# A two-layer trunk with mixers and experts: half of the second layer's modulation taken in one go between the layers

## The chip, the cores and the metric

The kernel runs on one core of a Trainium2 chip. The metric is the device time of one execution in microseconds, as the median of several runs. The profile is of one other execution. Engines are named as in the profile: PE is TensorE (PEld its weight loads), DVE is VectorE, ACT is ScalarE, POOL is GpSimd, SP is SyncE, which issues nearly all DMAs here.

## The reference

Two layers over 256 latent and 256 context tokens, 1024 wide, all in float32. Each layer has a token mixer with four branches and then a mixture of 16 experts, and both are fed by a modulated norm. Cut to what matters here:

```python
for l in range(2):
    mod_x = split((silu(c) @ ada_w[l] + ada_b[l]), 6)       # ada_w[l]: 1024 x 6144
    mod_c = split((silu(c_ctx) @ ada_w[l] + ada_b[l]), 6)
    hx, hc = [rms_norm(x, norm1_g[l]) * (1 + mod[1]) + mod[0] for each stream]
    mc, mx = token_mixer(hc, hx)        # column groups of w_in, two scans, convolution, attention, merge
    xx = xx + mod_x[2] * mx
    hx = rms_norm(xx, norm2_g[l]) * (1 + mod_x[4]) + mod_x[3]
    xx = xx + mod_x[5] * expert_choice_moe(hx)              # 16 experts, 32 tokens each
    # the context stream does the same in the first layer only
```

The six chunks of `mod` are 1024 columns each. Chunks 0 and 1 are needed at the start of a layer's mixer, chunk 2 at its end, and chunks 3, 4 and 5 in the experts.

## The kernel before

All of it stands in one instruction program. Loops are unrolled, and a planner in the compiler orders the instructions of each engine by its own reckoning of when their operands are ready, so that an engine's order can differ from the program text; on the chip each engine then runs its list in order and waits at the first instruction that is not ready. Memory on the chip is handed out by a small allocator (`Mem`, lines 252 to 323) that prefers the piece which has been free for longest.

A modulation chunk is a product of 8 weight tiles (128 x 1024, 512 KB each) with the two conditioning vectors. A tile is loaded by SyncE and used by four matmuls with 32 weight columns each (`Ada.step`, lines 463 to 473), which land in the PSUM tile `pa`; there is one such PSUM buffer. The profile counts a float32 matmul as two pieces, so a tile is 8 pieces of `pa`. After the eighth tile `mod_write` (lines 444 to 454) copies the sums out on VectorE (line 446), transposes them and adds the bias (line 453).

The first layer's chunks 1 and 0 run at the very start, from 16 buffers. The second layer's chunks 1 and 0 run in the background of the first mixer. Its chunks 2 to 5 are the matter here: they are 32 tiles, taken by an `AdaBack` with a pair of 1024-column buffers. It holds a credit, and each call `run(n)` adds n tiles of credit and issues whole tiles:

```python
nxt.append(AdaBack([(1, c) for c in range(2, 6)], keep))   # line 1664, last scatter of the experts
nxt[1].run(TR[0])                                          # line 1666: 0 tiles
ada_bg.run(TR[1])                                          # line 763: 2 tiles, ahead of the modulation
ada_bg.run(TR[2])                                          # line 767: half a tile, 8 times in its loop
ada_bg.run(ADA[l])                                         # line 806: 2 tiles at each weight block
ada_bg.run(SCN[l])                                         # line 934: half a tile per scan level
```

The order of the work around the change is this. The last expert of the first layer gets its weights (line 1608), its outputs are scattered into the token stream (lines 1646 to 1668), and `TokenSums` gathers the sums of squares beside them (lines 542 to 557). `reload` (lines 1670 to 1682) fetches small tables and the first two weight blocks of the next mixer. Then the second mixer begins: the token sums become a reciprocal root on VectorE (lines 498 to 504), it is broadcast by TensorE (line 590), and 16 steps of VectorE, ScalarE and GpSimd modulate the tokens (lines 774 to 780) into a high and a low part. The mixer's products start from these: a small one with `wa` (lines 1009 to 1014), then blocks of `w_in`, each loaded by SyncE (line 803) into one of three raw buffers and split by ScalarE (line 804) and VectorE (line 805). The blocks come in the order of lines 1019, 1022, 1041 (two), then five for the second recurrence with the scan of the first before them (line 1046). Line 1265 finishes what is left of the background ahead of the merge. The mixer's end fetches five tiles of the expert weights ahead (line 1260).

## Time and profile before

| | us |
|---|---|
| median of 3 runs | 2023.9 |
| lowest and highest run | 2020.21, 2026.08 |
| the profiled execution | 2021.9 |
| its span, first to last instruction | 2020.1 |
| TensorE busy | 1859.6 (92%) |
| VectorE busy | 801.5 (40%) |
| ScalarE busy | 526.1 (26%) |
| DMA queue of SyncE, share of 16 engines | 71.2% |
| mean granted TensorE clock, of full | 0.985 |

A slice of the page is a fortieth of the span, 50.5 us. The two stretches in which the DMA engines move 409 GB/s are the experts of the two layers; the second mixer lies between them, from about 1165 us on. A group or row with `pa` in this stretch belongs to the modulation product, `ada_w` to its loads, `wg` to weight blocks of the mixer, `moe_w` to expert weights. Busy matmuls are pipelined, so the busy time of a group can overlap with that of its neighbours.

### The profile page before, as it was taken

The numbers are of one execution on the slowest core, as the hardware profiler recorded it, in microseconds if no ns is written. First come the engines' busy times: TensorE is split into PE (matmuls) and PEld (weight loads), VectorE is DVE, ScalarE is ACT, GpSimd is POOL, SyncE is SP. The second block draws the span as 40 slices with busy tenths as digits, with TensorE's granted clock in tenths as the row PEclk, the third lists the DMA queues.
The fourth block names the chain that finished last, engine by engine and source line by source line (L and its number), as shares of the span: only waits on it lengthen the run. The fifth ranks groups of instructions, "written<-read, shape, count | busy, mean of one in ns | idle before, by whom it ended". The sixth has DMA issues, their size and how long they took to land.

```text
span 2020.1 us, 28474 instructions
## 1 busy us (share of the span) xinstructions
PE 1859.6 (92%) x11722; PEld 1089.5 (54%) x11722; DVE 801.5 (40%) x1768; ACT 526.1 (26%) x929; POOL 28.7 (1%) x52
## 2 busy tenths in 40 slices
PE   7999999999999899999897889999998999987877
PEld 3666677887887434434232356788997333221213
DVE  5464638837543313212020345769865111110101
ACT  4432336622232211101000243447443100000000
POOL 0000000000000000000000010001000000000000
PEclk9998999999999899999999999999998999999999
DMA  8744531322326999999999856334568999999999
GB/s 310 224 151 135 177 102 58 105 84 84 122 98 260 359 401 350 380 409 409 409 409 409 314 188 199 105 102 139 198 251 326 409 409 409 409 409 409 409 409 332
DMA packets 154005, 549.03 MB, mean 272 GB/s; under 512 B 11026, under 2 KB 22674, under 8 KB 153108
## 3 DMA queue, kind: packets, MB, share of 16 engines
q1 hardware_dynamic: 153300, 544.08, 71.2%
q0 software_dynamic: 576, 3.15, 0.5%
q8 instruction: 92, 1.51, 0.3%
q14 instruction: 37, 0.30, 0.0%
HBM read 544.03 MB, written 3.15 MB: 271 GB/s over the span
## 4 chain that ended last, share of the span: by engine, by line
PE 71%; DMA 20%; DVE 5%; issue 2%; ACT 2%; SPq 0%; DVEq 0%; ACTq 0%
PE pd L428 41%; PE ps L428 15%; DMA r<-moe_w 9%; DMA base<-moe_w 7%; PE pm L428 6%; PE pa L428 6%; DMA base<-ada_w 2%; PE pm L425 2%; DMA base<-wg 1%; ACT r L804 1%; PE ps L1597 1%; DVE r L805 1%; DMA base<-xT 0%; DVE r L1195 0%; DVE base L1594 0%
## 5 line engine op out<-in xcount | busy, mean ns | idle before, releaser
L428 PE MATMUL pd<-r 128*128 128x256 f32 (+3 forms) x2976 | 572.3, 363 | 12.0 <-DMA r<-moe_w 7.6
L428 PEld LDWEIGHTS pd<-r 128*128 128x128 f32 (+2 forms) x2976 | 424.7, 184 | 132.0 <-issue 59.3
L428 PE MATMUL pd<-r,r 128*128 128x512 f32 (+3 forms) x1304 | 284.1, 435 | 12.0 <-DMA r<-moe_w 9.4
L805 DVE TENSOR_TENSOR r<-base,r 128x1024 fp32r<-128x1024 f32 x136 | 166.0, 1222 | 160.5 <-ACT r L804 157.4
L428 PEld LDWEIGHTS pd<-r,r 128*128 128x128 f32 (+2 forms) x1304 | 162.7, 167 | 107.6 <-issue 59.3
L804 ACT ACTIVATE r<-base 128x1024 fp32r<-128x1024 f32 x136 | 143.5, 1059 | 268.9 <-PE pd L428 216.2
L428 PE MATMUL ps<-base 32*64 32x64 f32 (+12 forms) x2372 | 178.3, 280 | 12.3 <-DMA base<-hy 4.4
L428 PE MATMUL pd<-r,base 128*32 128x512 f32 (+1 forms) x680 | 166.7, 598 | 12.0 <-DMA r<-moe_w 10.4
L428 PEld LDWEIGHTS ps<-base 32*64 32x64 f32 (+7 forms) x2372 | 113.2, 144 | 73.3 <-issue 43.3
L428 PE MATMUL pm<-base 128*128 128x128 f32 (+12 forms) x660 | 104.7, 326 | 18.3 <-DVE base L1528 5.8
L428 PE MATMUL ps<-r,base 128*64 128x512 f32 (+4 forms) x468 | 98.6, 525 | 13.7 <-DVE base L1598 6.3
L428 PE MATMUL pd<-base 128*32 128x512 f32 (+1 forms) x408 | 100.5, 595 | 6.4 <-DMA base<-moe_w 5.6
L428 PEld LDWEIGHTS pm<-base 128*128 128x128 f32 (+5 forms) x660 | 72.2, 179 | 61.2 <-issue 31.5
L428 PEld LDWEIGHTS pd<-r,base 128*32 128x32 f32 (+1 forms) x680 | 42.0, 122 | 112.1 <-issue 73.9
L1594 DVE TENSOR_TENSOR r<-base,pd 64x512 f32<-64x512 f32 x16 | 10.9, 680 | 214.4 <-PE pd L428 202.2
L1593 ACT ACTIVATE base<-pd 128x512 f32<-128x512 f32 (+1 forms) x32 | 19.0, 594 | 253.7 <-PE pd L428 253.7
L1594 DVE TENSOR_TENSOR base<-base,pd 128x512 f32<-128x512 f32 x16 | 11.0, 688 | 184.6 <-PE pd L428 150.4
L428 PE MATMUL pa<-r,r 128*128 128x512 f32 (+1 forms) x384 | 82.6, 342 | 1.1 <-DVE base L866 1.1
L1644 ACT ACTIVATE base<-ps 32x512 f32<-32x512 f32 (+2 forms) x28 | 14.7, 526 | 252.5 <-PE ps L428 248.0
L1644 ACT ACTIVATE r<-ps 32x512 f32<-32x512 f32 (+2 forms) x32 | 15.4, 480 | 249.9 <-PE ps L428 243.8
L428 PE MATMUL pd<-base,r 128*32 128x512 f32 (+1 forms) x296 | 71.3, 597 | 9.4 <-DMA base<-moe_w 9.4
L428 PE MATMUL pa<-base 128*32 128x256 f32 (+1 forms) x704 | 70.1, 407 | 9.4 <-DMA base<-ada_w 9.2
(241 smaller groups left out, 1633.6 us busy)
## 6 DMA issues: line engine op xcount, KB each, us to landing
r<-moe_w SPq DMA_DIRECT2D x251, 1024.0 KB, 18.2
base<-moe_w SPq DMA_DIRECT2D x131, 1024.0 KB, 17.9
base<-wg SPq DMA_DIRECT2D x152, 512.0 KB, 3.3
base<-ada_w SPq DMA_DIRECT2D x84, 512.0 KB, 4.6
r<-ada_w SPq DMA_DIRECT2D x12, 512.0 KB, 10.3
base<-xT SPq DMA_DIRECT2D x4, 1024.0 KB, 6.2
filters<-r SPq DMA_DIRECT2D x8, 256.0 KB, 4.3
base<-filters POOLq DMA_DIRECT2D x2, 1024.0 KB, 6.4
```

The costliest lines, as they stand in the source:

```text
L425: T.transpose(out, in_, ident)
L428: return T.matmul(out, lhsT, rhs, start=start, stop=stop, **kw)
L804: A.activation(w[0](), raw(), AF.Copy)
L805: V.tensor_tensor(w[1](), raw(), F(w[0]()), op=OP.subtract)
L1593: A.activation(s_(np_=rows), pa[0:rows, :], AF.Silu)
L1594: V.tensor_tensor(h_(np_=rows), s_(np_=rows), pb[0:rows, :], op=OP.mult)
L1597: T.transpose(p[:, q * rows:q * rows + rows], h_(q * 128, n=128, np_=rows), cs("ident", n=rows, np_=rows))
L1644: A.activation(dst, src, AF.Copy)
```

## The change

Chunks 2 and 3 of the second layer leave the background. A new class takes them: at the end of the first layer's experts it gets as many free 1024-column buffers as there are, up to eight, and issues their loads at once; in the second mixer, after the broadcast of the reciprocal root and ahead of the modulation loop, it issues the matmuls of all 16 tiles, and behind each tile the load that takes its buffer next. After it, chunks 4 and 5 go to a pair of buffers in the background, at one tile per weight block where it was two, and with no call in the modulation loop. The weight slots and the saved tokens are given back ahead of the new buffers.

```diff
--- before.py
+++ after.py
@@ -25,11 +25,10 @@
 BASE = 52736 - RA - RB
 ENGS = ('AV', 'AVG')
 
-TR = (0, 2, 0.5)
 SCN = (0.5, 0.5)
 FL = (1, 1)
 DAS = (0.5, 1)
-ADA = (2, 2)
+ADA = (2, 1)
 FIRST = ("gk", "gq")
 AHEAD = ((0, 0), (0, 5))
 
@@ -494,6 +493,34 @@
                 if not self.left:
                     self.buf.free()
 
+    class AdaTurn:
+
+
+        def __init__(self, chunks, bufs):
+            self.tiles, self.bufs, self.issued = [(l, c, k) for l, c in chunks for k in range(KB)], bufs, 0
+            for _ in bufs:
+                self.load()
+
+        def load(self):
+            if self.issued < len(self.tiles):
+                l, c, k = self.tiles[self.issued]
+                S.dma_start(out=self.bufs[self.issued % len(self.bufs)](),
+                            in_=ins["ada_w"][l][128 * k:128 * k + 128, c * 1024:(c + 1) * 1024])
+                self.issued += 1
+
+        def run(self):
+            for i, (l, c, k) in enumerate(self.tiles):
+                if k == 0:
+                    p = ps("a")
+                b = self.bufs[i % len(self.bufs)]
+                for j in range(4):
+                    mm(p[32 * j:32 * j + 32, 0:256], cs_b(k * 32, n=32), b(j * 256, n=256), k == 0, k == KB - 1)
+                self.load()
+                if k == KB - 1:
+                    mod_write(l, c, p)
+            for b in self.bufs:
+                b.free()
+
 
     def rsqrt_small(x, n, y, t):
 
@@ -760,11 +787,10 @@
             b = rs_tokens(sums.tokens(mem), 2, mem)
             rs = bcast_rs(b, 2)
             b.free()
-            ada_bg.run(TR[1])
+            ada_bg.run()
+            ada_bg = AdaBack([(1, 4), (1, 5)], mem.take(2048))
         for k in range(KB):
             t = tmp[k % 2]
-            if l:
-                ada_bg.run(TR[2])
             for s in range(2):
                 c = slice(s * 256, s * 256 + 256)
                 sc_, sh = Ac(k * 2 + s, n=1), mod[l](k * 2 + s, n=1)
@@ -1656,14 +1682,11 @@
                                            op0=OP.mult, op1=OP.add)
                 if not last and gr == 3:
                     if d == 0:
-                        b, keep = [b for b in slots if b.mem is mem][:2]
+                        b = [b for b in slots if b.mem is mem][0]
                         slots.remove(b)
                         spare.append(b)
-                        slots.remove(keep)
                         nxt.append(TokenSums(0, [view(b, 512 * i, 512) for i in range(4)], tag="s"))
-                        nxt.append(AdaBack([(1, c) for c in range(2, 6)], keep))
                     nxt[0].step(d)
-                    nxt[1].run(TR[0])
                 if last and gr == 3:
                     S.dma_start(out=outT[:, d * 256:d * 256 + 256], in_=xk(d, 1))
 
@@ -1690,7 +1713,18 @@
                     gather(gr + 1)
             if gr < 3:
                 scatter(gr)
-        for b in spare + slots + mid + [xg[1]] + gone + Pg + ys:
+        for b in slots + gone:
+            b.free()
+        mem.merge()
+        if not last:
+            bufs = []
+            while len(bufs) < KB:
+                try:
+                    bufs.append(mem.take(1024))
+                except MemoryError:
+                    break
+            nxt.append(AdaTurn([(1, 2), (1, 3)], bufs))
+        for b in spare + mid + [xg[1]] + Pg + ys:
             b.free()
         mem.merge()
         dump(f"xmoe{l}", xb[0]())
```

## Rows read from the trace of the kernel before

**Rows 1.** The page, slices of the span: busy tenths of TensorE; GB/s of the DMA engines.

```profile
PE   7999999999999899999897889999998999987877
...
GB/s 310 224 151 135 177 102 58 105 84 84 122 98 260 359 401 350 380 409 409 409 409 409 314 188 199 105 102 139 198 251 326 409 409 409 409 409 409 409 409 332
```

**Rows 2.** Busy time by stretch: length, PE, PEld, DVE, ACT, POOL, clock, DMA share, GB/s.

```profile
1166.00:1180.00 14.00, 13.27 (x75) 4.18 (x68) 12.44 (x30) 7.75 (x17) 6.44 (x6) 0.89 0.68 219
1138.00:1150.00 12.00, 11.91 (x120) 7.86 (x120) 5.91 (x23) 5.79 (x14) 0.00 (x0) 1.00 0.98 303
1157.00:1186.00 29.00, 25.26 (x139) 9.71 (x138) 18.71 (x51) 9.22 (x19) 6.44 (x6) 0.88 0.61 200
1186.00:1273.00 87.00, 81.33 (x918) 57.40 (x916) 41.81 (x102) 34.68 (x66) 1.46 (x5) 1.00 0.55 183
1273.00:1340.00 67.00, 66.48 (x590) 54.51 (x587) 42.72 (x108) 28.95 (x61) 2.14 (x5) 1.00 0.27 95
```

**Rows 3.** Busy time by stretch of tile pa alone: PE, PEld, DVE, then as above.

```profile
1157.00:1186.00 29.00, 7.38 (x64) 2.32 (x64) 0.43 (x1) 0.88 0.61 200
1186.00:1273.00 87.00, 17.19 (x192) 4.51 (x192) 0.84 (x2) 1.00 0.55 183
...
1166.00:1186.00 20.00, 4.82 (x44) 1.27 (x36) 0.43 (x1) 0.93 0.57 184
```

**Rows 4.** TensorE's waits, 1157 to 1273 us: us in total, times, longest.

```profile
PE pa L428 <- DMA base<-ada_w: 4.5, 5, 2.2
```

**Rows 5.** Groups of TensorE, 1186 to 1273 us: count, busy, mean ns, idle before.

```profile
L428 PE MATMUL pa<-base 128*32 128x256 f32 x192 | 17.3, 390 | 3.8 <-DMA base<-ada_w 3.8
```

**Rows 6.** Timeline, 1157 to 1201 us: start, us, engine, line, count, idle before.

```profile
1157.22 0.84 PE L428 MATMUL pa<-base 128*32 128x256 f32 x10
...
1165.25 1.26 DVE L774 SCALAR_TENSOR_TENSOR base<-base,pm 128x256 f32<-128x256 f32 x3 [1.21 <-PE pm L425]
...
1179.60 0.43 DVE L446 COPY base<-pa 128x256 f32<-128x256 f32 x1 [1.32 <-PE pa L428]
1179.94 0.48 DVE L780 SCALAR_TENSOR_TENSOR r<-base,r 128x256 fp32r<-128x256 f32 x1
...
1191.30 2.36 DVE L805 TENSOR_TENSOR r<-base,r 128x1024 fp32r<-128x1024 f32 x2 [3.38 <-ACT r L804]
...
1200.67 0.64 PE L428 MATMUL pa<-base 128*32 128x256 f32 x8 [2.19 <-DMA base<-ada_w]
```

**Rows 7.** SyncE's DMA issues in order of time, 1142 to 1186 us.

```profile
1141.78 0.85 SPq L1681 DMA_DIRECT2D base<-wg  x2
1142.68 0.42 SPq L1682 DMA_DIRECT2D base<-cn  x1
1143.20 1.52 SPq L466 DMA_DIRECT2D base<-ada_w  x2
1157.21 0.33 SPq L803 DMA_DIRECT2D base<-wg  x1
```

**Rows 8.** SyncE's own waits, 1140 to 1290 us.

```profile
SPq L466 <- PE pa L428: 50.7, 24, 6.6
```

**Rows 9.** Loads of ada_w, 1140 to 1290 us.

```profile
DMA to landing us min/median/max: 3.6/4.6/8.6
```

**Rows 10.** Busy time at the kernel's start, columns as in rows 2.

```profile
22.00:24.00 2.00, 2.00 (x11) 0.56 (x11) 0.08 (x1) 0.27 (x1) 0.00 (x0) 1.00 1.02 408
```

**Rows 11.** Timeline of TensorE at the kernel's start: four tiles in a row.

```profile
38.85 1.91 PE L428 MATMUL pa<-base 128*32 128x256 f32 x32
```

**Rows 12.** Busy time by stretch, around 1162 us, columns as in rows 2.

```profile
1162.00:1164.00 2.00, 0.00 (x0) 0.00 (x0) 1.65 (x11) 0.00 (x0) 0.00 (x0) 0.53 0.96 352
1168.00:1170.00 2.00, 2.00 (x5) 0.73 (x5) 2.00 (x6) 1.72 (x5) 0.87 (x1) 0.76 0.90 332
```

**Rows 13.** The chain in order of time: start, us, what.

```profile
1185.30 4.83 DMA base<-wg
...
1785.73 19.76 DMA r<-moe_w
```

## The prediction

> **What bounds the kernel now.** I read the slices of the page first, then busy time by stretch, the tiles of the modulation product, TensorE's waits, a timeline, SyncE's issue order, and last the chain. TensorE is busy nearly everywhere; the DMA engines are full only while expert weights stream [rows 1]. Between lies the stretch that the change touches, from the first layer's last expert into the second mixer, 1138 to 1340 us. There TensorE is busy 81.3 of 87 us and then 66.5 of 67 while the DMA moves 183 and 95 GB/s [rows 2]: the stretch is TensorE's, and memory has room. Its holes are 29.0 - 25.3 = 3.7 us in 1157 to 1186 and 87.0 - 81.3 = 5.7 us in 1186 to 1273 [rows 2].
>
> The 32 weight tiles of the four modulation chunks (4 matmuls each, seen as 8 pieces) run here: 64 pieces, 8 tiles, before 1186 and 192 pieces, 24 tiles, after it [rows 3]. TensorE stood idle 4.5 us in five waits for such a tile [rows 4], 3.8 us of it after 1186 [rows 5]; the longest, 2.19 us before 1200.67, is one tile with mixer matmuls queued behind it [rows 6]. The reason is the pair of buffers: SyncE issues two tiles at 1143.20 and nothing more until 1157.21 [rows 7], because the next load wants a buffer that TensorE must read first; this kind of wait makes 50.7 us of SyncE's time [rows 8]. One tile takes 3.6 us at least and 4.6 us in the median from issue to landing [rows 9].
>
> **The change part by part.** No matmul, byte or vector instruction is added or removed: 32 tiles and four chunk ends before and after. What moves is when 16 of them run.
>
> *The turn.* Chunks 2 and 3 get every free 1024-column piece, up to eight. I count six: the buffer of the saved tokens has 4096 columns (four pieces), and the weight slot that the pair no longer takes gives two. Six loads then stand behind the reload of the small tables, where now two stand [rows 7]. From 1138 to 1150 the DMA moved 303 GB/s [rows 2]. Four more tiles are 2.1 MB, 5 us at the 408 GB/s that the kernel's first 16 tiles reach [rows 10]: all six land about 1156, before TensorE first has time for one at 1157.22 [rows 6]. The loads cost nothing there; the scatter is what hides them, and without it TensorE would wait those 5 us.
>
> *What it costs TensorE ahead of the mixer.* Eight tiles more than now fall before 1186. A tile run without waits costs 1.91 / 4 = 0.48 us [rows 11]; mixed with other shapes its busy time is 17.19 / 24 = 0.72 us, part of it shared with neighbours [rows 3]. I take 0.55, nearer to the pure one: 8 x 0.55 = 4.4 us added. Two things hide it. One is the 3.7 us of holes [rows 2], above all 1162 to 1164, where no matmul runs while VectorE takes a reciprocal root [rows 12]. The other is the clock: from that hole on it is granted at 0.53, and back at 0.76 in 1168 to 1170 [rows 12], so at the half level, 1.2 GHz, for some 7 us (the mean of 0.88 over 29 us [rows 2] says the same: 2 x 0.12 x 29). Some 5 us of them are busy, and the full level would give back up to 2.5 us. I take 3.0 us hidden in holes and 1.2 us from the clock: +0.2 us net. Bounds: -1.8 (all holes and the whole clock) and +4.4 (nothing hidden).
> The Trainium skill ("TensorE: Matmul & The Clock Gate", Part 1: The HAM clock gate) says that the throttled clock is the default and that activity releases it. The fall behind the hole agrees; no row shows whether these 32-column tiles, put into the hole, hold the clock. By the rule the clock term would be the full 2.5 us and this part -1.1 us.
>
> *The second round of the ring.* Tiles 7 to 16 are loaded only as TensorE frees one of the six buffers, from about 1157.8 on. With the two weight blocks of that place (one stands at 1157.21 [rows 7]) that is 12 x 0.524 = 6.3 MB, 15.4 us at 408 GB/s, and some 3 us until the first lands: the last tile is there about 1176. The modulation's last step ends at 1180.4 [rows 6], and the mixer's first product needs it, so a wait for a late tile mostly falls where TensorE cannot finish anyway. Lower bound 0. Upper bound: if all ten tiles stand ahead of the mixer's matmuls, the other work that TensorE does from 1166 to 1180, 13.3 us [rows 2] less the 4.8 of the tiles [rows 3], is pushed behind, 8.5 us. I take 1.5 us, near the lower end, as the single tile waits are 2.2 us at most [rows 4].
>
> *The background half.* After 1186 there are 16 tiles where there were 24: 8 x 0.55 = 4.4 us less on TensorE (3.8 to 5.8 by the two tile prices). The 3.8 us of waits [rows 5] would be 2.5 us for 16 tiles in proportion; with one tile per weight block, not two, a pair of buffers has twice the time. I take 1.3 us left, 2.5 us saved (bounds 0 and 3.8). In program order both versions finish in the scan of the second recurrence, so nothing later changes.
>
> *The rest.* The calls inside the modulation loop and the zero-rate call in the last scatter go; they only issue tiles counted already. The end of the turn's second chunk, a copy of 0.43 us [rows 6] with two small adds, comes onto VectorE during the modulation, where it is busy 18.7 of 29 us [rows 2]: 0.3 us. The background pair is the same 2048 columns, so the five expert tiles fetched ahead in the mixer should stay.
>
> Sum: +0.2 + 1.5 - 4.4 - 2.5 + 0.3 = -4.9 us. Behind the stretch TensorE has hardly a hole until 1340 [rows 2]; then the expert weights stream at 409 GB/s [rows 1], and the chain ends on them [rows 13]. The stream starts as the mixer gives up its buffers, so it shifts with it and the gain passes through. The profiled execution took 2021.9 us, the span of 2020.1 and 1.8 around it; it would take 2017.0. The median shown, 2023.9, lies 2.0 us above it: 2019.0.
>
> **The rivals.**
> *The hole only moves* (16%). In 1186 to 1273 the tiles are also filler while VectorE runs the scan; if weight blocks are not ready in their place, TensorE idles instead. For it: a weight block needs VectorE before it can be used, 2.36 us for two [rows 6]. Against it: of TensorE's 5.7 us of holes there 3.8 are waits for tiles. It comes out the same if the planner of the instruction order spreads the turn as it spreads the tiles now, so that the change hardly does what it says. The 4.4 us are not won: -4.9 + 4.4 = -0.5, 2023.4 us.
> *More comes back* (20%). All holes and the whole clock ahead of the mixer (-1.8), no late tile (0), the upper tile price (-5.8) and all waits (-3.8) give, with the 0.3 of the copy, -11.1: 2012.8 us. For it: the late tile of 1200.67 also held up what was queued for the first scan.
> *The vector queue is caught* (15%). The end of a chunk is a VectorE copy that waits for the chunk's last tile, and VectorE runs in order. The copy of the first chunk at 1179.60 stands ahead of the last modulation step and made VectorE wait 1.32 us [rows 6]. If the copy of the turn's second chunk stands ahead of the first modulation step (1165.25), the mixer starts when that chunk is complete: at 1176 by the rate above, at 1181 by the 303 GB/s of the reload [rows 2], so 11 to 16 us late. Less the 6.9 us won behind it, that is +4 to +9, in the middle +6.5: 2030.4 us. It decides when the copy waits longer than 6.9 us. For it: in the program text the turn comes ahead of the loop. Against it: the one wait of this kind is short.
>
> *The issue queue is held* (7%). SyncE's ten new buffer waits stand ahead of weight blocks, as 24 waits of this kind do now, 6.6 us at the longest [rows 8]. If the block of 1185.30, which is on the chain [rows 13], comes that much later, it is -4.9 + 6.6 = +1.7: 2025.6 us. Against it: that block waits for the mixer's own first product, and by then the turn's loads are out.
> The Trainium skill ("DMA: Bandwidth & Descriptors", Anatomy of one DMA) has the rule behind this one: a semaphore wait is held on the issuing sequencer and not in the DMA engines. The 50.7 us of SyncE [rows 8] agree.
>
> **How the numbers follow.** About 0.3% (6 us) is what a measurement of this kernel can tell from no change. The forecast holds 42%; its own range, 2014 to 2023, lies on both sides of that bound: 0.19 faster, 0.23 same. The moved hole gives 0.14 same and 0.02 slower (if the ring stalls besides), the larger gain 0.20 faster, the vector queue 0.12 slower and 0.03 same, the issue queue 0.06 same and 0.01 slower. So faster 0.39, same 0.46, slower 0.15. The range, 2011 to 2030, takes in the larger gain whole and half of the vector queue.
>
> **What would show it.** Right: six loads of modulation weights back to back behind the table reload; 16 tiles (128 pieces) before 1186; a shorter clock fall at 1162; fewer and shorter waits for tiles after 1186; the mixer's work after 1200 some 5 us earlier. Wrong: a first modulation step later than 1166 with a chunk's copy ahead of it on VectorE, TensorE waiting more than 3 us for tiles 7 to 16, or idle time in the scan where tiles were.

## The result: 0.6% slower, and the profile after

The changed kernel takes 2034.9 us (median of 8 runs, 2032.65 to 2040.02), the kernel before in the same runs 2023.56 (2016.96 to 2029.6). The ratio is 1.0061, with a 95% interval of 1.0044 to 1.0079. The forecast was 2019.0 and its range ended at 2030: the sign was wrong.

Where the loss arises is read by the start of the same instruction in both traces, counted from the first modulation step (line 774 before):

| instruction | start before | later by |
|---|---|---|
| first result of the mixer leaves PSUM (L1016) | 1185.3 | 1.7 |
| value pair leaves PSUM (L840) | 1203.5 | 7.4 |
| gate of the third recurrence (L1089, last) | 1288.0 | 3.2 |
| attention, first and last row maximum (L1209) | 1367.8, 1411.8 | 3.4, 5.5 |
| merge (L1341) | 1472.9 | 5.2 |
| merged product split (L1364, last) | 1521.6 | 10.5 |
| last scatter of the experts (L1594) | 2002.1 | 10.5 |

So it has three parts: some 3 us in the start of the mixer, where 5 were to be won, 2 us in the attention, and 5 us between 1473 and 1522, where nothing was expected. One trace is not exact to better than 3 us: two of the programs below, table_in_the_way and filters_moved, run the instructions of the kernel before in the same order up to about 1360, and at 1288 they stand 0.4 us earlier and 2.9 us later. Four traces have the full turn and one tile per block, and differ ahead of 1288 in little but addresses: they stand 3.2, 2.2, 3.4 and 1.7 us later (changed, filters_back, layout_kept, kept_but_filters). So the start loses some 2 us rather than 3; that the 5 were not won is sure.

The stretches from 1157 to 1273 as in [rows 2], after the change, and the tiles `pa` alone as in [rows 3]; line 428 before is line 427 now, lines 803 to 805 are 829 to 831:

```profile
1157.00:1186.00 29.00, 26.03 (x174) 9.36 (x166) 17.53 (x49) 7.78 (x17) 5.54 (x7) 1.00 0.66 219
1186.00:1273.00 87.00, 78.42 (x852) 57.91 (x851) 40.55 (x95) 36.20 (x67) 1.44 (x5) 0.96 0.45 152
```

```profile
1157.00:1186.00 29.00, 9.36 (x104) 2.66 (x96) 0.42 (x1) 1.00 0.66 219
1186.00:1273.00 87.00, 12.73 (x144) 3.34 (x144) 0.84 (x2) 0.96 0.45 152
```

Ahead of 1186 the clock no longer falls (1.00, where [rows 2] had 0.88) and 104 pieces run where 64 did. Behind it 48 pieces are gone and 4.5 us of tile time with them (one more tile runs at 1273.33, just outside; with it, it is 40 pieces and 4.0 us), yet TensorE is idle 87.0 - 78.4 = 8.6 us instead of 5.7, and its clock is down 0.04 x 87 = 3.5 us, as much as in the fall at 1162 before (0.12 x 29 = 3.5). In this trace the fall has not gone. It came 37 us later (the clock is 0.51 from 1162 to 1169 before, 0.50 from 1199.4 to 1206.2 after). The place is not fixed by the program alone: filters_moved, in the old order, falls a little in both stretches:

```profile
1157.00:1186.00 29.00, 23.91 (x129) 8.90 (x122) 18.02 (x49) 9.23 (x19) 6.43 (x6) 0.94 0.60 200
1186.00:1273.00 87.00, 81.44 (x891) 57.50 (x890) 40.36 (x99) 34.65 (x66) 1.44 (x5) 0.98 0.55 182
```

TensorE's waits between 1157 and 1273, the two longest lines (compare [rows 4]); the wait for tiles is down from 4.5 to 1.4 us, and a new one, for a block's split, is longer:

```profile
PE pd L427 <- ACT r L830: 2.6, 1, 2.6
PE pa L427 <- DMA base<-ada_w: 1.4, 2, 1.2
```

SyncE's issues, start and length (compare [rows 7]; L507 is the turn, L465 the background, L829 a weight block), and its waits from 1140 to 1190:

```profile
1142.69 34.63 SPq L507 DMA_DIRECT2D base<-ada_w  x16
1177.37 0.90 SPq L465 DMA_DIRECT2D base<-ada_w  x2
1186.16 0.33 SPq L829 DMA_DIRECT2D base<-wg  x1
1192.54 0.33 SPq L465 DMA_DIRECT2D base<-ada_w  x1
1192.97 0.37 SPq L829 DMA_DIRECT2D base<-wg  x1
```

```profile
SPq L507 <- PE pa L427: 21.2, 9, 5.8
SPq L829 <- PE pd L427: 7.8, 1, 7.8
```

All 16 tiles of the turn stand in one run of 34.6 us. Behind it comes a block that must wait 7.8 us for a product of TensorE, because its raw buffer holds `wa` (it waited 5.4 us before, too), then a tile of the background that waits until 1192.54 for one of the pair's buffers, and only behind that the next block. Before, a block left at 1157.21 [rows 7], and these two ahead of the one of 1185.30 [rows 13]:

```profile
1159.61 0.38 SPq L803 DMA_DIRECT2D base<-wg  x1
...
1174.93 0.33 SPq L803 DMA_DIRECT2D base<-wg  x1
```

What becomes of the late blocks is seen on ScalarE. L830 (L804 before) is the split of a block, the 128x1024 lines L1059 to L1062 (L1033 to L1036 before) are the gate of the first scan with two table loads. After:

```profile
1193.43 0.38 ACT L1049 ACTIVATE base<-pd 128x256 f32<-128x256 f32 x1 [3.47 <-PE pd L427]
...
1195.44 1.05 ACT L830 ACTIVATE r<-base 128x1024 fp32r<-128x1024 f32 x1
...
1197.53 1.07 ACT L1059 ACTIVATE base<-base 128x1024 f32<-128x1024 f32 x1
1198.47 1.07 ACT L830 ACTIVATE r<-base 128x1024 fp32r<-128x1024 f32 x1
1199.56 1.28 ACT L1060 ACT_TABLE_LOAD   x1
```

Before:

```profile
1190.21 2.01 ACT L804 ACTIVATE r<-base 128x1024 fp32r<-128x1024 f32 x2 [1.72 <-DMA base<-wg]
...
1194.67 1.08 ACT L1033 ACTIVATE base<-base 128x1024 f32<-128x1024 f32 x1
1195.77 1.28 ACT L1034 ACT_TABLE_LOAD   x1
```

Both blocks of the value pair were split ahead of the gate; now the second one is split inside it. The landing is not all of it: the first block took 3.2 us to land and was there at 1189.3, and ScalarE stood idle for 3.47 us before 1193.43, but in its list the split stands behind that line. Busy time of 1196 to 1205 (columns as in [rows 2]), before and after:

```profile
1196.00:1205.00 9.00, 6.80 (x62) 5.64 (x61) 2.59 (x4) 5.04 (x5) 0.00 (x0) 1.00 0.67 221
```

```profile
1196.00:1205.00 9.00, 5.62 (x57) 3.78 (x50) 3.87 (x4) 8.83 (x13) 0.31 (x1) 0.69 0.88 300
```

ScalarE is busy 8.83 of 9 us, TensorE is idle for 3.4 of them, and the granted clock is 0.69, so for part of the time at the half level of 1.2 GHz. The chain that ended last (start, us, what) runs through ScalarE's list from 1194.3 to 1202.1:

```profile
1197.65 0.94 ACT base L1059
1198.59 0.94 ACT r L830
1199.56 1.28 ACT L1060
...
1236.94 6.34 DMA base<-wg
```

A block's landing is on it only at 1236.94.

The late part: SyncE's issues of expert tiles fetched ahead (L1286, L1260 before, five of them) and of the sixth (L1597, L1571 before). After:

```profile
1468.25 12.44 SPq L1286 DMA_DIRECT2D base<-moe_w  x5
1480.74 1.58 SPq L829 DMA_DIRECT2D base<-wg  x3
1482.44 0.38 SPq L1597 DMA_DIRECT2D base<-moe_w  x1
```

Before:

```profile
1429.35 0.38 SPq L1571 DMA_DIRECT2D base<-moe_w  x1
...
1444.48 0.38 SPq L1260 DMA_DIRECT2D base<-moe_w  x1
...
1468.34 0.38 SPq L1260 DMA_DIRECT2D base<-moe_w  x1
...
1472.71 2.87 SPq L1260 DMA_DIRECT2D base<-moe_w  x3
```

Five tiles leave in one run, and three blocks queue behind it. The allocator hands out other addresses in the second mixer, since six buffers of the turn are taken and given back there and the pair is taken later. The convolution's filter table now lies at column 10928, where the first of the five tiles goes, and its second table (`df` in the program, called the difference buffer in the expectations) at 23728, inside a weight slot. Not all of the 5 us need be this: from 1473 to 1522 the granted clock is 0.93 after and 0.97 before, so up to 0.04 x 49 = 2.0 us of it is clock.

### The profile page after: what moved, and what is told of

The parts are those of the page before. It is cut to its first block, busy times and chain, and to the rows that moved or that the text cites. A ratio compares the mean times of both kernels' runs of the same rounds, so it can differ in the third digit from the quotient of the medians.

```text
span 2030.9 us, 28467 instructions
## 1 busy us (share of the span) xinstructions
PE 1864.0 (92%) x11722; PEld 1095.0 (54%) x11722; DVE 802.4 (40%) x1768; ACT 526.3 (26%) x929; POOL 28.7 (1%) x52
## 4 chain that ended last, share of the span: by engine, by line
PE 70%; DMA 19%; DVE 6%; ACT 3%; issue 3%; SPq 0%; DVEq 0%; ACTq 0%
PE pd L427 41%; PE ps L427 15%; DMA r<-moe_w 9%; PE pm L427 6%; DMA base<-moe_w 6%; PE pa L427 5%; DMA base<-wg 2%; PE pm L424 2%; DMA base<-ada_w 1%; ACT r L830 1%; DVE r L831 1%; PE ps L1623 1%; DVE base L967 0%; DVE r L1221 0%; DVE base L969 0%
## 5 line engine op out<-in xcount | busy, mean ns | idle before, releaser
L830 ACT ACTIVATE r<-base 128x1024 fp32r<-128x1024 f32 x136 | 143.4, 1058 | 272.3 <-PE pd L427 217.3
L427 PE MATMUL pd<-r,base 128*32 128x512 f32 (+1 forms) x680 | 167.0, 597 | 13.0 <-DMA r<-moe_w 10.5
L427 PE MATMUL ps<-r,base 128*64 128x512 f32 (+4 forms) x468 | 99.0, 526 | 13.3 <-DVE base L1624 6.3
L427 PE MATMUL pd<-base,r 128*32 128x512 f32 (+1 forms) x296 | 71.3, 597 | 10.4 <-DMA base<-moe_w 10.4
## 6 DMA issues: line engine op xcount, KB each, us to landing
r<-moe_w SPq DMA_DIRECT2D x251, 1024.0 KB, 18.2
```

What stands on the lines that cost most here:

```text
L427: return T.matmul(out, lhsT, rhs, start=start, stop=stop, **kw)
L830: A.activation(w[0](), raw(), AF.Copy)
```

## The experiments

Every kernel was timed in five rounds beside the kernel before. "Later by" is read from one trace as above, at L840, at L1089 (1288) and at the end. "Split" says whether ScalarE splits both blocks of the value pair ahead of the first 128x1024 line of the gate. The expectations count their shift at 1288 from the last scatter ahead of the mixer, not from the first modulation step; the two differ by half a microsecond at most. A median is over 6 to 12 runs and a trace is one of them, so the two need not agree.

| kernel | median us | ratio, 95% | later by, us | split |
|---|---|---|---|---|
| changed | 2034.9 | 1.0061 [1.0044, 1.0079] | 7.4, 3.2, 10.5 | inside |
| layout_kept | 2026.47 | 1.0012 [0.9999, 1.0025] | 8.8, 3.4, 5.3 | inside |
| table_in_the_way | 2027.41 | 1.0013 [0.9997, 1.0030] | -1.2, -0.4, 0.6 | ahead |
| filters_back | 2033.64 | 1.0048 [1.0028, 1.0068] | 7.0, 2.2, 6.1 | inside |
| filters_moved | 2026.17 | 1.0008 [0.9990, 1.0025] | 2.4, 2.9, 4.4 | ahead |
| kept_but_filters | 2029.77 | 1.0025 [1.0010, 1.0041] | 7.3, 1.7, 5.2 | inside |
| blocks_first | 2029.49 | 1.0035 [1.0017, 1.0053] | 4.2, 2.7, 10.7 | ahead |
| layout_and_blocks | 2029.98 | 1.0021 [1.0004, 1.0037] | 7.3, 2.4, 3.0 | inside |
| ring_on_pool | 2033.15 | 1.0050 [1.0028, 1.0071] | 15.1, 8.8, 10.5 | ahead |
| blocks_on_pool | 2026.29 | 1.0007 [0.9991, 1.0024] | 9.8, 8.1, 9.5 | ahead |
| ring_reused | 2014.24 | 0.9949 [0.9931, 0.9968] | -1.8, -6.9, -6.2 | ahead |
| ring_waits_only | 2016.6 | 0.9953 [0.9930, 0.9976] | -3.1, -6.9, -7.0 | ahead |
| ring_bytes_only | 2022.9 | 0.9984 [0.9966, 1.0001] | 4.6, 3.2, 4.0 | inside |
| pace_two | 2037.08 | 1.0070 [1.0043, 1.0098] | 14.9, 14.0, 13.3 | inside |
| pace_alone | 2036.47 | 1.0046 [1.0024, 1.0068] | -3.2, 6.6, 7.2 | ahead |
| one_chunk | 2024.31 | 0.9994 [0.9976, 1.0012] | -1.2, 0.4, -0.8 | ahead |
| six_tile_turn | 2034.07 | 1.0050 [1.0031, 1.0070] | 4.0, 4.8, 6.5 | inside |
| background_on_pool | 2033.23 | 1.0040 [1.0019, 1.0061] | 8.3, 5.2, 6.4 | ahead |
| before_background_on_pool | 2030.79 | 1.0034 [1.0014, 1.0054] | 1.1, 10.2, 10.4 | ahead |

### Addresses

**layout_kept** is the changed kernel with every buffer of the second mixer at the address that it has in the kernel before.

```diff
+            mem.plan = [tuple(e) for e in PLAN]      # sizes and addresses of the kernel before
-            ada_bg = AdaBack([(1, 4), (1, 5)], mem.take(2048))
+            ada_bg = AdaBack([(1, 4), (1, 5)], ada_bg.keep)
```

> The changed kernel with one thing undone: every buffer that the second layer takes stands at the address it had before the change (the turn's six buffers and the background pair too), so only the turn, its order and the pace are new. Theory A (the loss comes in two places: about 2.4 us where the weight blocks queue behind the turn's loads on SyncE, and 7.5 us later, after 1375 us, because the buffers moved and the filter table of the convolution now stands where the first expert tile is fetched ahead): the later part goes, about 2026 us, ratio to before 1.001; the first fetched-ahead expert tile is issued near 1447 us and not near 1468, and the shift against the kernel before stays at +2.4 us from 1290 us to the end. Rival B (the turn itself causes all of it, the later loss follows from a TensorE that comes late): about 2035 us, ratio 1.006, the shift grows to +9.7 us at 1525 us as in the changed kernel.

The edit does two small things besides: the sums of a chunk are copied into a part of an older buffer, and the turn's buffers are not given back. With that the mixer's first result comes 4.9 us late instead of 1.7, which is made up by 1288.

The ratio falls from 1.0061 to 1.0012, and the late part is gone: from 1473 to 1522 the shift moves from 4.9 to 5.2. The expert tiles leave one by one again (L1611 is the sixth, L1300 the five):

```profile
1435.82 0.38 SPq L1611 DMA_DIRECT2D base<-moe_w  x1
...
1450.95 0.38 SPq L1300 DMA_DIRECT2D base<-moe_w  x1
...
1474.83 0.38 SPq L1300 DMA_DIRECT2D base<-moe_w  x1
```

The early part (3.4 at 1288) stays. So 0.5% of the time, some 10 us by the ratios (0.0049 x 2024) and 5 by the traces, is addresses and the order that the planner makes of them. Which addresses was then tried four ways: the table alone, and the pair of buffers put back, put in the way, and put in the way of layout_kept.

```diff
 # table_in_the_way: the kernel before
+        H = mem.take_span(10928, 2048) if l else mem.take(2048)
 # filters_moved: the kernel before; kept_but_filters: the same two in layout_kept
+        df, H = (mem.take_span(23728, 1024), mem.take_span(10928, 2048)) if l else ...
 # filters_back: the changed kernel
+        df, H = (mem.take_span(14256, 1024), mem.take_span(20656, 2048)) if l else ...
```

> The kernel before with one thing of the change done: in the second layer the filter table of the convolution (2048 columns) is taken at the address of the first expert tile that is fetched ahead, as in the changed kernel. Theory A: that load waits for the convolution's last read of the table, near 1467 us instead of 1444, the fetched-ahead tiles and the weight blocks of the last two merges crowd each other, about +5 us: 2028.5 us, ratio 1.0025. Rival B: the load has room to come late, 2023.6 us, ratio 1.000.

> the changed kernel with two buffers of the second layer's convolution at the addresses that they have in the kernel before (filter table 20656, its difference buffer 14256), nothing else moved. Theory A (the two lie on the first fetched-ahead expert tile and on a weight slot, so loads wait for the convolution): the five expert tiles leave one by one before 1473 again, the late step of +5.3 us between 1473 and 1522 goes, time about 2029.5 (ratio 1.0035). Rival (the late step comes from another buffer of the layout or from the changed order): step stays, time 2034.5 (ratio 1.006).

> the kernel before with the same two buffers of the second layer at the addresses of the changed kernel (filter table 10928, difference buffer 23728); no other instruction or address differs. Theory A: the late step of +5 us appears in the kernel before, time about 2028.5 (ratio 1.0025). Rival (the table alone moved cost 0.2 us in the trace; the pair is no different): time 2023.6 (ratio 1.000).

> layout_kept with the convolution's filter table and difference buffer at the changed kernel's addresses (10928 and 23728), and the two small buffers that stood there swapped into their places; everything else is as in layout_kept. Theory A (these two buffers make the late step): the step of about 5 us between 1473 and 1522 comes back, time about 2031 (ratio 1.0035). Rival (the rest of the layout, and the order of instructions that follows from it, is what layout_kept mended): no late step, time 2026.5 (ratio 1.001).

In the trace the table alone does next to nothing (0.6 us at the end), though four of the five tiles leave late and in one run there too, from 1467.73; its ratio fits both zero and the 1.0025 that was expected. In filters_back the late step is gone from the trace (6.2 at 1473, 5.3 at 1522), but the ratio falls by 0.0013 only. The pair put in the way costs 0.0008 and, against layout_kept, 0.0013 of the time, each within the uncertainty of its comparison, and the late step that was expected does not appear in either trace: filters_moved stands 4.1 us later at 1473 and 4.3 at 1522, kept_but_filters 4.0 and 4.1. (Their clock between the two is 1.00 where the kernel before has 0.97, which may hide up to 0.03 x 49 = 1.5 us.) All three ratios have the sign of the theory and a third to a half of the size that was expected, a sixth to a quarter of the 0.0049: the two filter buffers are at most a part of what the addresses cost, and the rest of it is not placed.

### The weight blocks and SyncE's queue

**blocks_first** splits the first two blocks and issues the next two ahead of the turn's second round; **layout_and_blocks** does that in layout_kept.

```diff
+            for i in range(2):
+                A.activation(ring[i][0](), raws[i](), AF.Copy)
+                V.tensor_tensor(ring[i][1](), raws[i](), F(ring[i][0]()), op=OP.subtract)
+            for i, n in enumerate(("gv1", "hq0")):
+                S.dma_start(out=raws[i](), in_=ins["wg"][l, BIDX[n]])
```

> The changed kernel with one thing undone: the split of the first two weight blocks and the loads of the two blocks that follow into their raw buffers are issued ahead of the turn's tiles 7 to 16, so that they don't queue behind ten buffer waits on SyncE; addresses as in the changed kernel. Theory A (queue order is the early loss): the first split block of the value pair is in use some 6 us earlier, the early shift of +2.4 us goes to 0 or below, about 2031 us, ratio 1.004. Rival C (the early loss is the turn's bytes and matmuls themselves, not the order): no change against the changed kernel, about 2035 us, early shift +2.4 us.

> Both undone at once: addresses as before the change, and the two weight blocks ahead of the turn's second round. Theory A: early and late loss are gone and only what the turn wins is left, 2018 to 2023 us, ratio 0.997 to 1.000. Rival B (the turn is the cause of all): 2031 to 2035 us. Rival C (order doesn't matter): as layout_kept, about 2026 us.

Two blocks ahead do not do it in the traces: the rest of the blocks still stands behind the ten loads, and the start of the mixer gains 1 us at most. The ratio of blocks_first is 0.0026 below the changed kernel's, as its theory A had it, but its trace is no sooner at the end (10.7 us), and layout_and_blocks is not below layout_kept. Next the ring's ten loads (**ring_on_pool**) or four blocks (**blocks_on_pool**) went to GpSimd's queue.

```diff
-                S.dma_start(out=self.bufs[...](),                 # ring_on_pool
+                (S if self.issued < len(self.bufs) else G).dma_start(out=self.bufs[...](),
-                S.dma_start(out=raw(), in_=ins["wg"][l, BIDX[name]])    # blocks_on_pool
+                (G if l and ri[0] <= 6 else S).dma_start(out=raw(), in_=ins["wg"][l, BIDX[name]])
```

> layout_kept with the turn's tiles 7 to 16 issued from GpSimd's queue; the first six stay on SyncE, every buffer and every instruction of the other engines is unchanged. Theory B (the ten buffer waits on SyncE's queue hold back the weight blocks): SyncE reaches the third to sixth block before 1180 instead of 1186, the +7 to +16 us that layout_kept shows at the copies and splits of 1200 to 1235 fall to under +3, the mixer starts at least 2 us earlier than in layout_kept (shift at 1288 from +3.3 to about 0), and the time is about 2022.5 (ratio 0.9985 to 1.0000). Rival (the turn's bytes or its TensorE work, which the queue does not change): the blocks leave early and land late, shift at 1288 stays above +2.5, time 2026 (ratio 1.001).

> layout_kept with the loads of the third to sixth weight block of the second mixer issued from GpSimd's queue instead of SyncE's; bytes, TensorE's work and the turn's ring stay as they are. Theory B (the ten buffer waits on SyncE's queue hold the blocks back): the third and fourth block leave before 1165 and the fifth and sixth by 1186, where layout_kept has 1190 to 1203; TensorE's idle time and clock fall of 1196 to 1211 shrink to under half, the shift at 1288 goes from +3.3 to 0 or below, time about 2022.5 (ratio 0.9995). Rival (the turn's bytes or its TensorE work, which stay): shift at 1288 stays above +2, time 2026 (ratio 1.001).

Both missed, and neither is a clean test: the wait moved to another engine's list. In ring_on_pool the modulation steps of GpSimd stand behind the loads, which wait 29.4 us for TensorE, and the last modulation step is 12 us late. In blocks_on_pool the blocks leave at 1158.65 and 1160.60, but ScalarE's split of one stands ahead of the modulation and waits for its landing:

```profile
1168.30 1.06 ACT L844 ACTIVATE r<-base 128x1024 fp32r<-128x1024 f32 x1 [8.41 <-DMA base<-wg]
```

Then the ten loads were taken apart, and in all three kernels chunks 2 and 3 are computed from incomplete weights: no loads (**ring_reused**), the loads' waits without their bytes, the bytes without waits for TensorE.

```diff
-                self.load()                                        # ring_reused
 # ring_waits_only: tiles 7 to 16 as 8 columns
+                o, n = (0, 1024) if self.issued < len(self.bufs) else (768, 8)
 # ring_bytes_only: matmuls on buffers 0 to 2, tiles 7 to 16 into 3 to 5
+                S.dma_start(out=self.bufs[i if i < n else n // 2 + i % (n // 2)](),
+                b = self.bufs[i % (len(self.bufs) // 2)]
```

> layout_kept with tiles 7 to 16 of the turn not loaded (their matmuls run on what stands in the six buffers, so the modulation of chunks 2 and 3 is left wrong): 5.2 MB and all ten buffer waits are gone, the matmuls stay. Theory B: SyncE is free from 1150 on, the blocks leave as in the kernel before or earlier, the predicted gain on the background half (fewer tiles behind 1186) shows, shift at 1288 about -4, time about 2019.5 (ratio 0.998). Rival (TensorE's pieces ahead of the mixer cost what the waits seem to): shift at 1288 above +2, time 2026 (ratio 1.001).

> layout_kept with the turn's tiles 7 to 16 loaded as 8 columns each instead of 1024, into the last quarter of the buffer (the rest of these tiles is stale, so chunks 2 and 3 are left wrong): the ten loads wait for TensorE and stand ahead of the weight blocks on SyncE's queue as before, but move 41 KB instead of 5.2 MB. If the waits on the queue cost: the third block leaves at about 1180, shift at 1288 of about +2 and a time of 2025.5 (ratio 1.001), near layout_kept. If the bytes cost: shift at 1288 about -6, time 2015 (ratio 0.996), near ring_reused.

> layout_kept with all bytes of the turn but no wait for TensorE: the matmuls of all 16 tiles use the first three buffers (so chunks 2 and 3 are left wrong), and tiles 7 to 16 are loaded in full into the other three, which nobody reads; these loads wait only for one another. If the waits on the queue cost: SyncE reaches the third block by 1165, shift at 1288 about -6, time 2015 (ratio 0.996). If the bytes cost: blocks land late though they leave early, shift at 1288 of +2 or more, time 2025.5 (ratio 1.001).

Without the loads the change is what was forecast and more: 6.9 us earlier at 1288, ratio 0.9949. With the waits alone it is the same, as was expected if the bytes cost. But it is no clean test of the waits: the planner made another order of it, with blocks between the loads. SyncE in ring_waits_only (L522 is the turn, L844 a block):

```profile
1146.61 22.41 SPq L522 DMA_DIRECT2D base<-ada_w  x11
1169.11 0.38 SPq L844 DMA_DIRECT2D base<-wg  x1
1171.13 1.28 SPq L522 DMA_DIRECT2D base<-ada_w  x3
1172.46 0.42 SPq L844 DMA_DIRECT2D base<-wg  x1
```

Two blocks stand within the turn's loads, and ScalarE splits the pair at 1192.36 and 1194.08, ahead of the gate at 1197.59. In ring_bytes_only SyncE is through with the turn by 1173.8, 12 us sooner than its first block could leave, and does not use it, because the order behind the turn is the changed kernel's. Its issues, and its waits from 1174 to 1190:

```profile
1173.81 0.91 SPq L479 DMA_DIRECT2D base<-ada_w  x2
1187.33 0.33 SPq L844 DMA_DIRECT2D base<-wg  x1
```

```profile
SPq L844 <- PE pd L439: 12.6, 1, 12.6
```

The blocks with free buffers stand behind the one that waits for TensorE, the splits fall inside the gate, and in its trace the mixer is 3.2 us late at 1288 as in layout_kept. (Its median says less: the ratio of 0.9984 lies about halfway between layout_kept and ring_reused.) By the words of their expectations both tests come out for the bytes. But the bytes are through when the blocks are held: the DMA engines then move 26 GB/s (columns as in [rows 2]).

```profile
1180.00:1187.00 7.00, 7.00 (x28) 2.75 (x26) 0.48 (x1) 0.51 (x1) 1.55 (x2) 1.00 0.07 26
```

So what the bytes change is above all the planner's order, and the waits need not cost where blocks stand between them.

The loss goes with the place of the blocks. In the eight kernels with an "inside", L840 loses 3.6 to 11.2 us against the copy of L1023 just ahead of it (5.3 in the changed kernel, 4.5 in layout_kept). In ten of the eleven with an "ahead" it stands between 3.1 earlier and 1.1 later; blocks_first, with 4.9 later, is the exception. That the split itself is the cause is not shown, and in half of the eight it can't be all: the chain of the changed kernel, filters_back, ring_bytes_only and six_tile_turn runs through ScalarE's gate and split there, but that of layout_kept, kept_but_filters, layout_and_blocks and pace_two runs past it, over the landing of a background tile. In layout_kept:

```profile
1200.72 4.25 DMA base<-ada_w
```

What the two have in common is SyncE's list: late blocks in one, a late tile in the other. Moving the split alone was not tried.

### The pace and the size of the turn

**pace_two** undoes the pace in layout_kept; **pace_alone** makes one and a half of the two in the kernel before, with its addresses and no turn (chunk sums copied as in layout_kept).

```diff
-ADA = (2, 1)     # pace_two
+ADA = (2, 2)
-ADA = (2, 2)     # pace_alone, the kernel before
+ADA = (2, 1.5)
```

> layout_kept with two tiles of the background per weight block instead of one: the background's 16 tiles then ride on the first eight blocks of the mixer. Prediction's term (half the pieces between 1186 and 1273 saves 4.4 us of TensorE and 2.5 us of waits): at two per block as many pieces stand there as before, and the shift at 1288 rises by 4 to 7 us over layout_kept's +3.3, time about 2030 (ratio 1.003). Rival (TensorE is waiting there anyway, for blocks, so the pieces fit into its gaps): shift at 1288 within 1 us of layout_kept, time 2026 (ratio 1.001).

> the kernel before, addresses kept, with one and a half background tiles per weight block instead of two and no turn. If tiles between blocks on SyncE's queue are what the pace saves (pace_two lost 10 us against layout_kept): time 2020 (ratio 0.998). If the pace only matters behind a held queue: 2023.5 (ratio 1.000).

pace_two loses 10.6 us at 1288 against layout_kept, more than the 4 to 7 expected; TensorE is busy 41.5 of 49 us behind 1186 at a clock of 0.83. But pace_alone is a miss of the other sign: it is 3.2 us earlier at L840 and 6.6 later at 1288. SyncE shows why:

```profile
1207.03 29.33 SPq L479 DMA_DIRECT2D base<-ada_w  x9
1236.46 11.22 SPq L844 DMA_DIRECT2D base<-wg  x3
```

Nine tiles in a row, each waiting for one of two buffers. The block behind them left at 1220.20 in the kernel before, 54.9 us after the first modulation step; here it is 62.1 us, 7.1 more (this whole trace stands 9.2 us later at that step). A slower pace does not help where it makes the planner put tiles together.

**one_chunk** and **six_tile_turn** take chunk 2 alone in the turn. (In one_chunk the pair's memory is also that of two of the six buffers, so tiles 7 and 8 land on tiles 1 and 2 before these are read, and chunk 2 is not computed.)

```diff
-            ada_bg = AdaBack([(1, 4), (1, 5)], ada_bg.keep)
+            ada_bg = AdaBack([(1, 3), (1, 4), (1, 5)], ada_bg.keep)       # ADA = (2, 1.5)
-            turn = AdaTurn([(1, 2), (1, 3)], six)
+            turn = AdaTurn([(1, 2)], six + pair)       # one_chunk; six_tile_turn: six alone
```

> layout_kept with a turn of one chunk only, its eight tiles in the six buffers and the two of the background pair, all loaded ahead and none behind a buffer wait; the other three chunks, 24 tiles, in the background at one and a half tiles per weight block. Theory B: no second round, so SyncE is free for blocks from 1150 on, shift at 1288 about -1 (24 tiles behind 1186 as in the kernel before, but fewer per block), time 2022.5 (ratio 0.9995), if anything the version that beats both. Rival (what counts is how many tiles stand between blocks on SyncE's queue behind 1186, as pace_two showed): shift at 1288 of +5 or more, time about 2030 (ratio 1.003).

> one_chunk with eight separate uses of six buffers: the turn takes chunk 2 alone, six tiles ahead and only the last two behind a buffer wait; chunks 3 to 5 in the background at one and a half tiles per weight block. If the second round's length is the cost (ring_reused, without it, won 9 us): SyncE reaches the third block by 1165, shift at 1288 about 0, time 2023 (ratio 0.9995), against 2026.5 of layout_kept. If any turn ahead of the mixer costs: 2026 or more (ratio 1.001).

Two buffer waits instead of none, and the ratio goes from 0.9994 to 1.0050. In one_chunk SyncE issues two blocks at 1156.20 right behind the eight tiles. Its clock falls in the hole at 1163, as in the kernel before, and it is back at 1.00 in 1187 to 1193, where TensorE runs without a gap; six_tile_turn keeps the clock in the hole and loses it behind. Two windows of one_chunk, then two of six_tile_turn (columns as in [rows 2]):

```profile
1163.00:1169.00 6.00, 4.41 (x9) 1.73 (x9) 4.79 (x14) 2.92 (x7) 0.88 (x1) 0.50 0.01 3
...
1187.00:1193.00 6.00, 6.00 (x47) 4.16 (x45) 2.20 (x3) 3.57 (x6) 0.00 (x0) 1.00 0.73 255
```

```profile
1163.00:1169.00 6.00, 6.00 (x33) 1.90 (x31) 3.71 (x9) 1.96 (x5) 1.66 (x2) 1.00 0.33 92
...
1187.00:1193.00 6.00, 2.01 (x42) 1.08 (x34) 1.76 (x2) 5.97 (x8) 0.00 (x0) 0.82 0.71 252
```

In the last one ScalarE is busy 5.97 of 6 us, again with a block's split inside the gate.

**background_on_pool** and **before_background_on_pool** load the background's tiles from GpSimd's queue, in layout_kept and in the kernel before.

```diff
-            S.dma_start(out=b(), in_=ins["ada_w"][self.l]...)
+            (G if bgq[0] else S).dma_start(out=b(), in_=ins["ada_w"][self.l]...)
```

> layout_kept with the 16 background tiles (chunks 4 and 5) loaded from GpSimd's queue; the turn and all blocks stay on SyncE, bytes and TensorE's work stay. If what holds the blocks behind 1186 are the background's buffer waits between them on SyncE's queue: blocks follow each other as raw buffers come free, the half clock at 1196 to 1211 goes, shift at 1288 from +3.3 to about 0, time 2022.5 (ratio 0.9995). If it is the turn's ten loads alone: SyncE still reaches the third block at about 1186, shift at 1288 stays at +2 to +4, time 2026 (ratio 1.001).

> the kernel before with the background tiles that the weight blocks and the scan call for loaded from GpSimd's queue instead of SyncE's; nothing else differs. If buffer waits on SyncE's queue cost blocks in the kernel before too: its 5.7 us of TensorE holes of 1186 to 1273 shrink by about 3, time 2020.5 (ratio 0.9985), and this version beats both. If the blocks there are bound by their splits: 2023.5 (ratio 1.000).

With all background waits off SyncE the third block of background_on_pool leaves at 1188.93, behind the turn as before. The next one leaves right after it, at 1189.35, 22.2 us after the first modulation step where it is 29.2 in layout_kept. The third block waits for the product with `wa`; what held the fourth was a background tile's wait. That was one of the two theories, but nothing is won by it, and both kernels are slower than without the move: TensorE now waits for the tiles, from 1186 to 1290 for 4.1 us where it is 1.9 in layout_kept, and for 7.8 us where it was 3.8 in the kernel before. The chain of before_background_on_pool has a tile with 9.46 us from its issue on GpSimd's queue to its landing (8.6 was the longest in [rows 9]); TensorE is busy 5.86 of 10 us behind it, at 0.78:

```profile
1221.01 9.46 DMA base<-ada_w
```

```profile
1225.00:1235.00 10.00, 5.86 (x49) 3.10 (x48) 2.92 (x10) 1.47 (x2) 1.06 (x2) 0.78 0.46 154
```

No version that computes everything beats the kernel before.

## Why the prediction was wrong

**What held.** The fall of the clock at 1162 went, six loads stood back to back, and the turn was paid ahead of the mixer: +0.2 + 1.5 + 0.3 was predicted for it, and the mixer's first result is 1.7 us late. That this sum fits is in part luck. 13 tiles stood ahead of 1186, not 16, so tile time there grew by 2.0 us and not 4.4; holes hid 0.8 us and not 3.0; and the clock came back whole (1.00), where half of it was taken. Behind 1186 tile time fell by 4.5 us (4.4 predicted), waits for tiles by 2.4, from 3.8 to 1.4 (2.5 predicted).

**The step that failed first** is *the background half*: it took 6.9 us of TensorE's tile time and waits for 6.9 us of the mixer. The tiles and their waits went as predicted, but the mixer came 3.2 us late at 1288 instead of 4.9 early, because the stretch filled with other idle time (7.2 us that are not waits for tiles, where it was 1.9) and a clock fall (up to 3.5 us). Roughly, -4.5 - 2.4 + 5.3 + 3.5 = +1.9 us, for the 3.2 - 1.7 = 1.5 in the trace. The forecast's opening, that the stretch is TensorE's, was true of the old order only. In the new one TensorE waited for others: in the changed kernel for ScalarE's list with the late splits (1194.3 to 1202.1), in layout_kept for a background tile. That both come from the new order of SyncE's list fits the traces, blocks_first excepted; no run shows it in which that order alone was changed.

**The rivals that came nearest.** *The hole only moves* (16%) has what TensorE shows: tiles were filler, weight blocks were not ready in their place, and TensorE idled. It looked for the reason in VectorE and priced it at 4.4 us. *The issue queue is held* (7%) has the reason, at 6.6 us for one block. It was dismissed with "that block waits for the mixer's own first product, and by then the turn's loads are out". The block does wait for that product (7.8 us, until 1186.16). What was overlooked is that three other blocks left ahead of it, two of them before 1160, and that these would now stand behind it. The Trainium skill ("DMA: Bandwidth & Descriptors", Anatomy of one DMA) says that a semaphore wait is held on the issuing sequencer; the 12.6 us wait of ring_bytes_only, with free buffers queued behind it, agrees.

**The second failure** is "the five expert tiles fetched ahead in the mixer should stay" and "nothing later changes". The pair has the same 2048 columns but at another address, and with it the buffers of the whole second mixer moved. layout_kept shows 0.5% of the time for this. It was costed at nothing without a look at where the buffers would come to lie.

**Left open:** why the filter buffers give back only a part of what layout_kept does; whether ScalarE's order or the late blocks and tiles cost the start of the mixer; and a version with the turn and early blocks that computes everything. The 2 us in the attention (1368 to 1412) are not shown to be the change's: its clock there is 0.96 (0.04 x 44 = 1.8 us), but so it is in filters_moved, which has the old order up to about 1360, while the kernel before and table_in_the_way have 1.00.

## What to carry to other kernels

When loads that wait for buffers are moved forward, list which loads stood ahead of them on the queue, not only the one on the chain: those with free buffers pay. Freeing or taking a buffer in one place changes every later address, so compare the addresses of later prefetches before costing the rest at nothing, and keep them fixed when testing the change itself. A time saved on the busiest engine counts only if its next input comes earlier too.

## What the runs showed of the hardware

The spread between runs of one kernel goes with the granted clock: of 26 runs of the kernel before, 2015.69 us had a mean of 0.991 and 2032.88 us one of 0.982, and 0.009 x 2020 is 18.2 for the 17.2 us between them. Most of what differs ahead of the change arises in the first 400 us: the half-level stretches in the traces lose some 10 us there before, 9 after, 2 in ring_reused and 19 in pace_alone. Hence all times here are medians of many runs, and traces are compared from a common instruction on. In the changed kernel the clock stayed at 1.00 where the hole at 1162 was filled and fell 37 us later, where TensorE stood idle 3.4 of 9 us; layout_kept, with the same turn, has 0.94 and 0.96 in the two stretches (1157 to 1186, 1186 to 1273), the kernel before 0.88 and 1.00, filters_moved 0.94 and 0.98. So filling a hole moved the fall in one trace, and one trace is not enough to count on it.
